# Decoder step on one core: nine pairs of the input projection by seven products instead of eighteen single tiles, with the sums of x formed beside the attention

## The chip, the cores and the metric

The kernel runs on one core of a Trainium2 chip. The metric is the time of one execution on the device in microseconds (us); the median of several runs is given, and one further execution was recorded by the hardware profiler. The engines are named as in the profile: PE (matrix products) with PEld (its weight loads), DVE (vector engine), ACT (scalar engine), POOL (GpSimd) and SP, which here only starts DMA transfers. POOL starts DMA transfers too; such an issue counts as busy time of POOL, one on SP does not count as busy time.

## The reference

One layer of a decoder for 512 prompt tokens and 8 decode tokens (520 in all), width 2048. Everything is float32.

```
def mixer(xn, conv_prev, gla_prev, w_in, conv_w, gate_w2, gate_b, gla_norm_g, w_out, chunk):
    proj = xn @ w_in
    bg, cg, hin, q, k, v, og, glr = jnp.split(proj, [...], axis=-1)
    cu, conv_new = causal_dwconv(cg * hin, conv_prev, conv_w)
    ya = bg * cu
...
    o, s_new = gla_chunked(qh, kh, vh, lf, gla_prev.astype(f32), chunk)
    o = o * lax.rsqrt(var + EPS) * gla_norm_g...
    yb = (o.reshape(...) * jax.nn.silu(og.astype(f32))).astype(xn.dtype)
    out = jnp.concatenate([ya, yb], axis=-1) @ w_out
    return out, conv_new, s_new

def conv_ffn(xn, prev, w_up, conv_w, conv_b, w_down):
    u, v = jnp.split(xn @ w_up, 2, axis=-1)
    cu, new = causal_dwconv(u, prev, conv_w)
    h = jax.nn.silu(cu + conv_b) * v
    return h @ w_down, new
```

`x + mixer(rmsnorm(x))`, then `x + conv_ffn(rmsnorm(x))`, then a last RMSNorm. `bg`, `cg`, `hin` and `og` are 1024 columns of `w_in` each, so eight tiles of 128 columns each.

## The kernel before

**Numbers and tiles.** A float32 product is made of three products of halves: each operand is split into a high part (rounded, written by ACT) and a low part (the rest, written by DVE), and PE adds hi·hi, hi·lo and lo·hi. Activations lie with the width on 128 partitions and the 520 tokens along the row, in two halves of 260 tokens (`HT`).

**Direct groups.** `group()` (L134) makes one tile of 128 output columns from all 16 tiles of the width: 16 tiles × 3 products × 2 token halves = 96 matmuls of 260 columns.

**Seven products.** The output projection ("wo"), the up projection ("up") and the down projection ("down") take a 2 × 2 block (two column tiles or chunks, two halves of the inner width, two token halves) by seven products instead of eight, after Winograd and Strassen. The weights are summed for it on the way (`weights`, `prepare`: three or four DVE additions per group, of which one is in some groups an adding DMA `raw<-raw` that POOL starts), and each of the seven needs its own hi (ACT) and lo (DVE, L1086) of 128 × 1024. The activations are needed in sums too, called forms 1 to 7. One such group is 7 × 24 = 168 matmuls. In "wo" and "down" one operand's forms are written to memory (`g_d`, `f_d`) and loaded back by `load_form` (L612), four loads of 260 KB for each form, into a ring of eight homes (`slots`). In "up" the forms of the normalised x are held in place. The order of the products within a group is `ORDER` = 1, 5, 6, 2, 7, 3, 4.

**Stages.** First x is loaded, transposed and split. Then the attention runs, one head after another; it is cut into steps by generators, and `tick()` runs a step between the projection groups, so that PE alternates between both. Convolution tiles 0 to 3 (three groups each: `cg`, `hin`, `bg`) are made there too. Behind it come convolution tiles 4 to 7 and output gate tiles 0 to 7, twenty direct groups. `mixed_done` takes two finished tiles, forms their sums (`pair_sums`) and stores the forms of the mixer's output to `g_d`: 8 stores of 130 or 260 KB for each pair, all issued on POOL. Then "wo" (two halves of its inner width times four column groups, `(c, g)`), "up" (44 groups), "down", and the last norm.

**What sets the order.** From "wo" on one loop walks over all products i (`order`, j = i % 7 within the group n). It prepares weights two products ahead, finishes the product before (`chunk_finish`, `up_finish`), starts the loads of the next group's weights on SP, and lets generators (`steps`) run their parts at set places. `in_order` keeps POOL's and SP's instructions in program order; every engine works its own queue strictly from the front, so that an instruction that waits holds back all that stand behind it.

**Places that matter here.** `load_residual(g)` (L1225) loads the residual x into the four accumulators `acc[g, q]` of column group g of "wo" with four POOL loads of 260 KB; it is called for g = 0 ahead of the loop, and for the others at j = 4 of the group before. `chunk_finish` adds products onto them on DVE (L1277). The forms of "wo" for c = 0 are loaded between the output gate tiles (14 POOL loads after each of two of them), the first of c = 1 in the first group of "wo", the rest in its fourth group. In "down" `add_residual` (L1230) adds the residual into `acc` by four adding POOL DMAs; it runs at j = 5 of the four groups of c = 1, the last of them at (1, 3), where also the forms of the next c are loaded. With 14 form loads of "down" on POOL and 14 on SP the last "up" group prepares the next stage.

Of the kernel before, what the change touches and what calls it, by code (L numbers as in the profile page):

```python
# [37 lines left out]
def trunk_kernel(  # L38
# [99 lines left out]
    soon, queue = deque(), deque()  # L138
# [26 lines left out]
    def group(w, c0, acts):  # L165
        ps = new_mm()
        ws = [piece(w, k0, 8, c0, P) for k0 in (0, 8)]
        for k0 in range(0, KD, 4):
            span(ps, ws[k0 // 8], acts, k0, k0 // 8 * 8, 4, KD)
            tick()  # L170
        return ps
# [37 lines left out]
    t_d = dp.tile([3, 4, 2, P, T], F32, name="t_d")  # L209
    v_d = dp.tile([NH, NS, DV], F32, name="v_d")  # L210
# [420 lines left out]

    def pair_sums(he, h):
# [9 lines left out]
    with ExitStack() as mix:  # L642
        slots[:4] = [yt1] * 4
        even = {}

        def mixed(k):
# [3 lines left out]
            if k < KD // 2:  # L650
                even[k] = yt1.tile([P, T], F32, tag="yl3", name="ye")
# [31 lines left out]
        with ExitStack() as gl:  # L683
            gp = gl.enter_context(tc.tile_pool(name="gla", bufs=1))
# [254 lines left out]
            for h in range(NH):  # L939
                ps = group(w_in, 3584 + h * P, xa) if h else first[0]  # L940
# [22 lines left out]
            assert not queue, len(queue)  # L963

        yctx = ctx.enter_context(ExitStack())
        slots[4:14] = [yctx.enter_context(tc.tile_pool(name="yt2", bufs=1, side="right"))] * 10
        wxr = yctx.enter_context(tc.tile_pool(name="raw2", bufs=4, side="right"))
        for j in range(4, 8):
            conv_tile(j)

        for j in range(8):
# [7 lines left out]
            if 2 <= j < 6:  # L979
                for x in range(2 * j - 4, min(2 * j - 2, 7)):  # L980
                    load_form("wo", 0, x)

    bctx.close()

# [3 lines left out]
    wx = ctx.enter_context(ExitStack())  # L988
    wxp = wx.enter_context(tc.tile_pool(name="sums", bufs=2))
    slots[14:] = [yctx.enter_context(tc.tile_pool(name="yt3", bufs=1, side="right"))] * 2  # L990
# [10 lines left out]
    def first_tile(kind, g, m):  # L1001

        return 2 * g + 8 * m if kind == "wo" else 4 * g + 2 * m

# [5 lines left out]

    def source(kind, at):
        if kind == "up":
            return lambda m, k: up_source(*at, m, k)
# [37 lines left out]
    groups = [("wo", (c, g)) for c in range(2) for g in range(NG)]  # L1051
# [3 lines left out]
    NW = 7 * 2 * NG  # L1055
# [3 lines left out]
    def begin(n):  # L1059
        kind, at = groups[n]  # L1060

        state[kind, at] = weights(source(kind, at), kind == "up" or at[0] > 0)
# [29 lines left out]
    xq = {}  # L1092
# [26 lines left out]
    def up_finish(i):  # L1119
# [22 lines left out]
        elif r == 3:  # L1142
            add(z2, bk["f"], st["c"])
            if t >= 2:
                nc.vector.tensor_tensor(z2, z2, R[:, HT:], op=ALU.mult)

# [61 lines left out]

    def acc_tag(n):
        return f"x{'hl'[n % 2]}{8 + n // 2}"  # L1210

    def rows_of(d, kind, g, q):

        m, b = first_tile(kind, g, q // 2), q % 2
        return d[m : m + 2, :, b * HT : (b + 1) * HT].rearrange("m p c -> p m c")
# [82 lines left out]
    ssq = [cp.tile([P, T], F32, tag="glr", name="ssq"), R]  # L1298

    def form(f, g):  # L1300

        if f == 1:
            x = pair_tiles(bigA, f"b{g}")
        elif f in (2, 3):
            x = [
                bigA.tile([P, T], F32R, tag=acc_tag(4 * g + q), name="b2")
                for q in ((0, 3) if f == 2 else (1, 2))
            ]
        else:
            k = {5: 0, 4: 4, 6: 8, 7: 12}[f] + g  # L1310
            x = [slots[k].tile([P, T], F32R, tag=f"y{s}{k}", name=f"y{s}{k}") for s in "hl"]
        for j, q in enumerate(zip(*(halves(y) for y in x))):
            xq[f, 2 * g + j] = q
        return x
# [100 lines left out]
    in_order = InOrder(nc.gpsimd.engine, nc.sync.engine)  # L1415
    begin(0)
    load_rest(0)
    load_residual(0)
    prepare(0)
    prepare(1)  # L1420
    steps, seeded = [], {}
    for i, (kind, at, r) in enumerate(order):
# [6 lines left out]
        if i:  # L1429
            (up_finish if order[i - 1][0] == "up" else chunk_finish)(i - 1)  # L1430
# [201 lines left out]
```

## Time and profile before

| | us |
|---|---|
| median of 3 runs (2237.19 to 2238.16) | 2237.39 |
| the profiled execution, its own time | 2237.94 |
| its span (first to last instruction) | 2236.2 |
| PE busy / DVE / ACT / POOL | 2189.3 / 1634.4 / 1049.2 / 459.6 |
| start until the attention | 0 to 70 |
| attention with conv tiles 0 to 3 | 70 to 442 |
| conv tiles 4 to 7, output gate 0 to 7 | 442 to 684.6 |
| "wo" | 685.4 to 856.5 |
| "up" | 856.5 to 1755.6 |
| "down" | 1755.6 to 2166 |
| last part | 2166 to 2236 |

The page has its times in microseconds of the span. In a row of the timeline stand the start, the length of the run of instructions, the engine, the line, the operation, the names (out<-in) and their number; in brackets behind it how long the engine stood idle just before, and what ended that. In a table of windows stand the busy time of each engine in a stretch, with the number of instructions, then the clock that PE was granted (1 is full), the share of the DMA engines' time, and the bytes moved. A group of instructions has its count, its busy time, the mean of one in ns, and the idle time before them.

### The profile page before, as it was taken

To read this page: it belongs to the slowest core of one execution; us is meant where nothing else is said; L and a number is where in the kernel's file an instruction comes from. 1 tells how busy PE (TensorE), PEld (TensorE's weight loads), DVE (VectorE), ACT (ScalarE), POOL (GpSimd) and SP (SyncE) were. 2 spreads that over 40 slices of the span, in tenths; PEclk is the share of its full clock that TensorE was granted. 3 is DMA by queue.
4 is the path that set the end of the run, shared out by engine and by line. 5 is a ranking of instruction groups with operands and counts; after the bars stand their busy time and mean duration, and the time that the engine had idled before them with its cause. 6 is when DMAs were issued, how large, how long until landed. Compare 5 with 4: busy or idle time off the path is not lost.

```text
span 2236.2 us, 43928 instructions
## 1 busy us (share of the span) xinstructions
PE 2189.3 (98%) x17963; PEld 2165.8 (97%) x17963; DVE 1634.4 (73%) x2183; ACT 1049.2 (47%) x1504; POOL 459.6 (21%) x629
## 2 busy tenths in 40 slices
PE   8999999999999998999999999999999999999997
PEld 7998999999999997999999999999999999999997
DVE  5355364544457896888989898898888777777776
ACT  5334334322233485555555555555555554344445
POOL 3023142241333311211312122122121303100100
PEclk9999999999999998999999999999999999999999
DMA  8243353375588699566767667667676869976944
GB/s 248 83 132 98 112 151 107 107 195 129 156 263 253 214 258 288 153 175 165 189 172 183 182 163 195 174 175 185 166 187 194 287 189 224 290 216 179 285 118 152
DMA packets 461239, 413.33 MB, mean 185 GB/s; under 512 B 21177, under 2 KB 417365, under 8 KB 460893
## 3 DMA queue, kind: packets, MB, share of 16 engines
q1 hardware_dynamic: 418353, 285.89, 44.6%
q0 software_dynamic: 41360, 122.40, 21.6%
q8 instruction: 141, 2.31, 0.4%
q10 hardware_dynamic: 1324, 2.23, 0.3%
q14 instruction: 61, 0.50, 0.1%
HBM read 294.13 MB, written 79.25 MB: 167 GB/s over the span
## 4 chain that ended last, share of the span: by engine, by line
PE 84%; DMA 2%; DVE 2%; issue 1%; ACT 1%; SPq 0%; ACTq 0%; DVEq 0%
PE mm L1107 28%; PE mm L134 20%; PE ms L1107 11%; PE x L1259 8%; PE y L1259 8%; PE e L1259 3%; PE f L1259 3%; DMA raw<-in_w_down_dram 1%; PE ms L830 1%; DVE lo L1086 0%; DMA t_d<-t 0%; DVE s L1032 0%; DMA x_d<-acc 0%; PE ms L1533 0%; DMA raw<-in_w_out_dram 0%
## 5 line engine op out<-in xcount | busy, mean ns | idle before, releaser
L1082 ACT ACTIVATE hi<-raw 128x1024 fp32r<-128x1024 f32 x288 | 304.4, 1057 | 215.8 <-issue 71.9
L1107 PE MATMUL mm<-yl,hi 128*128 128x260 f32 x1408 | 398.9, 283 | 3.8 <-DVE yl L118 2.4
L1107 PE MATMUL mm<-yh,hi 128*128 128x260 f32 x1408 | 399.0, 283 | 1.4 <-DMA yh<-t_d 1.4
L1107 PE MATMUL mm<-yh,lo 128*128 128x260 f32 x1408 | 398.0, 283 | 0.0
L1086 DVE TENSOR_TENSOR lo<-raw,hi 128x1024 fp32r<-128x1024 f32 x288 | 351.9, 1222 | 45.9 <-ACT hi L1082 45.6
L1086 DVE TENSOR_TENSOR lo<-s,hi 128x1024 fp32r<-128x1024 f32 x216 | 265.5, 1229 | 116.9 <-ACT hi L1082 111.6
L1082 ACT ACTIVATE hi<-s 128x1024 fp32r<-128x1024 f32 x216 | 228.4, 1057 | 199.5 <-DVE s L1032 74.8
L1107 PEld LDWEIGHTS mm<-yl,hi 128*128 128x128 f32 x1408 | 266.2, 189 | 4.8 <-DVE yl L118 2.7
L1107 PEld LDWEIGHTS mm<-yh,hi 128*128 128x128 f32 x1408 | 265.4, 189 | 1.8 <-DMA yh<-t_d 1.8
L1107 PEld LDWEIGHTS mm<-yh,lo 128*128 128x128 f32 x1408 | 266.4, 189 | 0.0
L1107 PE MATMUL ms<-b,hi 128*128 128x260 f32 x1408 | 258.3, 284 | 0.0
L106 DVE TENSOR_TENSOR lo<-raw,hi 128x1024 fp32r<-128x1024 f32 x112 | 144.6, 1291 | 140.7 <-ACT hi L105 133.6
L105 ACT ACTIVATE hi<-raw 128x1024 fp32r<-128x1024 f32 x112 | 118.1, 1055 | 264.5 <-PE mm L134 220.6
L1107 PEld LDWEIGHTS ms<-b,hi 128*128 128x128 f32 x1408 | 219.0, 190 | 0.0
L1259 PE MATMUL y<-form,hi 128*128 128x260 f32 x1120 | 206.8, 285 | 3.1 <-DVE acc L1277 3.1
L1259 PE MATMUL x<-form,hi 128*128 128x260 f32 x1120 | 205.6, 284 | 3.4 <-DVE acc L1277 2.2
L1107 PE MATMUL ms<-b,lo 128*128 128x260 f32 x704 | 199.6, 284 | 0.0
L1036 POOL DMA_DIRECT2D raw<-raw x64 | 57.2, 894 | 651.0 <-DVE s L1032 481.6
L1032 DVE TENSOR_TENSOR s<-s,raw 128x1024 f32<-128x1024 f32 x144 | 176.0, 1222 | 2.5
L1259 PEld LDWEIGHTS y<-form,hi 128*128 128x128 f32 x1120 | 174.3, 190 | 3.6 <-ACT hi L1082 3.1
L1259 PEld LDWEIGHTS x<-form,hi 128*128 128x128 f32 x1120 | 173.0, 189 | 4.2 <-issue 1.9
L134 PE MATMUL mm<-xh,hi 128*128 128x260 f32 x768 | 160.7, 291 | 3.8 <-ACT xh L120 3.8
(328 smaller groups left out, 5570.5 us busy)
## 6 DMA issues: line engine op xcount, KB each, us to landing
raw<-in_w_up_dram SPq DMA_DIRECT2D x176, 512.0 KB
raw<-in_w_down_dram SPq DMA_DIRECT2D x96, 512.0 KB
raw<-in_w_in_dram SPq DMA_DIRECT2D x92, 512.0 KB
raw<-raw POOLq DMA_DIRECT2D x64, 512.0 KB, 6.2
form<-f_d SPq DMA_DIRECT2D x126, 260.0 KB
f_d<-t POOLq DMA_DIRECT2D x80, 260.0 KB, 5.6
raw<-in_w_out_dram SPq DMA_DIRECT2D x32, 512.0 KB
form<-g_d POOLq DMA_DIRECT2D x56, 260.0 KB, 7.4
```

The costliest lines, as they stand in the source:

```text
L105: nc.scalar.activation(hi, raw, AF.Copy)
L106: nc.vector.tensor_tensor(lo, raw, hi.bitcast(F32), op=ALU.subtract)
L134: nc.tensor.matmul(o, w, xx, start=first and i == 0, stop=last and i == 2)
L830: nc.tensor.matmul(pb[:, c * 64 : (c + 1) * 64], L[:, c, :], rhs[:, c], start=True, stop=True,)
L1032: return lambda: nc.vector.tensor_tensor(out, x, y, op=ALU.add)
L1036: return lambda: nc.gpsimd.dma_start(out, x, accum_op=ALU.add)
L1082: nc.scalar.activation(his[i], src, AF.Copy)
L1086: nc.vector.tensor_tensor(los[i], src, his[i].bitcast(F32), op=ALU.subtract)
L1107: nc.tensor.matmul(st["bank"][b], w[:, k, :], x, start=b not in st["used"] and k == 0 and j == 0, stop=k == 7 and j == 2, skip_group_check ...
L1259: nc.tensor.matmul(ps[:, m, :], w[:, k, m * P : (m + 1) * P], x, start=b not in st["used"] and k == 0 and j == 0, stop=k == 3 and j == 2, ...
```

## The change

Only output gate tiles 0 and 1 stay direct groups behind the attention. The other eighteen tiles (convolution tiles 4 to 7 with three each, gate tiles 2 to 7) become nine pairs of a new kind "mix", which the common loop runs ahead of "wo" with the same `up_product` as "up":

```
+    MIX = (
+        ("ch", 4), ("ch", 5), ("b", 4), ("og", 2), ("ch", 6), ("ch", 7), ("b", 6), ("og", 4),
+        ("og", 6),
+    )
...
-    groups = [("wo", (c, g)) for c in range(2) for g in range(NG)]
+    groups = [("mix", (n,)) for n in range(len(MIX))]
+    groups += [("wo", (c, g)) for c in range(2) for g in range(NG)]
```

For them the forms 4 to 7 of the scaled x are needed. `mixer_sums(g)` makes them for a quarter of the width, in four steps each that run after the groups from head 1 of the attention on. It loads x anew (POOL), scales it (ACT, eight half tiles), forms four sums (DVE) and splits them (ACT, DVE). For g = 0 the results stay on the chip; for g = 1, 2, 3 they go to memory (`mt_d`, 24 POOL stores) and come back through `load_mixer_sums` (24 POOL loads of 260 KB) once the attention's tiles, and for g = 3 the last direct tile's, are free.

```
+    def mixer_sums(g):
+        xg = [tmp()[:, :T] for _ in range(4)]
+        for q, x in enumerate(xg):
+            m = first_tile("mix", g, q // 2)
+            nc.gpsimd.dma_start(two(x), rows_of(xT_d, "mix", g, q))
+            for j, h in enumerate(halves(x)):
+                nc.scalar.activation(h, h, AF.Copy, scale=gmix[:, m + j : m + j + 1])
+        def out(f, t):
+            if g == 0:
+                split(t, *form(f, g))
+            else:
+                stored(t, [mt_d[f - 4, g, x] for x in range(2)], tmp())
+        yield
+        t1, t2 = xg[0], tmp()[:, :T]
+        sub(t1, xg[0], xg[1])
+        minus(t2, t1, xg[3])
+        out(5, t1)
+        yield
...
+    def load_mixer_sums(g):
+        for f in (5, 4, 7, 6):
+            for x, t in enumerate(form(f, g)):
+                nc.gpsimd.dma_start(t.bitcast(F32), mt_d[f - 4, g, x])
...
             for h in range(NH):
+                if h == 1:
+                    extra.extend(mixer_sums(g) for g in range(4))
...
-        for j in range(4, 8):
-            conv_tile(j)
-
-        for j in range(8):
+        for g in (1, 2):
+            load_mixer_sums(g)
+
+        for j in range(2):
...
+    load_mixer_sums(3)
```

`mix_finish` takes the results out of PE's banks (for "b" times the convolution's result, else times R), and `mix_gate` does the rest of a pair in steps during the next group: for "ch" the product of both tiles and the convolution, for "og" the Silu and the product with the attention's output, and for "b" and "og" the sums and stores to `g_d`:

```
+    def mix_gate(n):
+        st = state.pop(("mix", (n,)))
+        u, v = st[2], st[7]
+        what, j = MIX[n]
+        if what == "ch":
...
+        dst, i = g_d[k // 8], k // 2 % 4
+        t21, t34 = pair_sums(u, v)
+        yield 4.5
+        stored(halves(u)[0], [dst[6:7, x, i] for x in range(2)], fh())
+        yield 7
+        stored(v, [dst[4:6, x, i] for x in range(2)], fh())
+        yield 7.5
+        stored(t21, [dst[0:2, x, i] for x in range(2)], fh())
+        yield 10.5
+        stored(t34, [dst[2:4, x, i] for x in range(2)], fh())
```

In the common loop all 28 form loads of "wo", c = 0, move to the last "mix" group, all on POOL; the first residual load comes behind them; one form load of c = 1 moves from the first to the third group of "wo"; and `add_residual` for column group 1 moves from (1, 3) to (2, 2). Four matmuls that only mark banks are added at i = 0.

```
     in_order = InOrder(nc.gpsimd.engine, nc.sync.engine)
+    mult(R2, R, R)
     begin(0)
     load_rest(0)
-    load_residual(0)
...
-        if i == NW:
+        if i in (0, NW):
             x = xq[1, 0][0]
             for ps in [bank() for _ in range(4)]:
                 nc.tensor.matmul(ps[:, :HT], x[:, :P], x, start=True, stop=True)
...
-            if c == 0 and g == 0 and j == 0:
+            if c == 0 and g == 2 and j == 0:
                 load_form("wo", 1, 0)
...
-        if kind == "up" and at[0] == NF - 1:
+        if 7 * n in (NM - 7, NU - 7):
             for x in {1: (0, 1), 2: (2, 3), 4: (4, 5), 6: (6,)}.get(j, ()):
-                load_form("down", 0, x)
+                load_form(groups[n + 1][0], 0, x)
+        if i == NM - 1:
+            load_residual(0)
...
-            if c == 1 and j == 5:
-                add_residual((g + 2) % NG)
+            if j == 5 and (c, g) in ((1, 0), (1, 1), (1, 2), (2, 2)):
+                add_residual({0: 2, 1: 3}.get(g, c - 1))
```

Three places of the instruction order follow. First POOL behind the attention. Before the change the eight stores of the pair of convolution tiles 2 and 3 (`g_d`) are followed by form loads for "wo":

```order
L630 DMA g_d0_119<-t_4935 128x2x260
L612 DMA form_6812<-g_d0_119 128x2x260
L612 DMA form_6816<-g_d0_119 128x2x260
L612 DMA form_6820<-g_d0_119 128x2x260
L612 DMA form_6824<-g_d0_119 128x2x260
L612 DMA form_6972<-g_d0_119 128x2x260
```

With the change the same stores are followed by 24 loads from `mt_d`, eight for each of g = 1, 2, 3; the names yh, yl with a number are the places of the hi and lo parts. The last eight, for g = 3, are:

```order
L697 DMA yh3_5433<-mt_d_122 128x520
L697 DMA yl3_5434<-mt_d_122 128x520
L697 DMA yh7_5437<-mt_d_122 128x520
L697 DMA yl7_5438<-mt_d_122 128x520
L697 DMA yh15_5441<-mt_d_122 128x520
L697 DMA yl15_5442<-mt_d_122 128x520
L697 DMA yh11_5445<-mt_d_122 128x520
L697 DMA yl11_5446<-mt_d_122 128x520
```

The pair `yh3`, `yl3` is form 5 of g = 3: it stands seventeenth and eighteenth among the loads.

Second, POOL ahead of "wo". Before, the four loads of the residual (`acc`) follow the stores of one gate pair, and the 28 form loads stand between the gate tiles, in two runs of 14:

```order
L630 DMA g_d1_120<-t_7122 128x2x260
L1225 DMA acc_7566<-xT_d_116 128x2x260
L1225 DMA acc_7567<-xT_d_116 128x2x260
L1225 DMA acc_7568<-xT_d_116 128x2x260
L1225 DMA acc_7569<-xT_d_116 128x2x260
L612 DMA form_7630<-g_d1_120 128x2x260
L630 DMA g_d1_120<-t_7514 128x260
```

With the change they stand at the end of a run of 28 form loads with four stores among them, of which these are the last:

```order
L615 DMA form_7651<-g_d0_119 128x2x260
L615 DMA form_7715<-g_d0_119 128x2x260
L615 DMA form_7717<-g_d0_119 128x2x260
L615 DMA form_7719<-g_d0_119 128x2x260
L615 DMA form_7721<-g_d0_119 128x2x260
L1395 DMA acc_7723<-xT_d_116 128x2x260
L1395 DMA acc_7724<-xT_d_116 128x2x260
L1395 DMA acc_7725<-xT_d_116 128x2x260
L1395 DMA acc_7726<-xT_d_116 128x2x260
L633 DMA g_d1_120<-fh_7772 128x2x260
```

So `acc` is now the last of 36 issues that all belong to the last "mix" group.

Third, DVE in the first group of "wo". The first two additions onto `acc` (product 5, bank y) stand between the low parts (`lo`) of the weights for the coming products. Before:

```order
L1086 TENSOR_TENSOR lo_7699<-raw_7559,hi_7696 128x1024
L1277 TENSOR_TENSOR acc_7567<-acc_7567,y_7639 128x520
L1277 TENSOR_TENSOR acc_7569<-acc_7569,y_7639 128x520
L1086 TENSOR_TENSOR lo_7730<-s_7557,hi_7728 128x1024
L1277 TENSOR_TENSOR acc_7566<-acc_7566,e_7597 128x520
```

With the change:

```order
L1170 TENSOR_TENSOR lo_7856<-raw_7411,hi_7853 128x1024
L1447 TENSOR_TENSOR acc_7724<-acc_7724,y_7796 128x520
L1447 TENSOR_TENSOR acc_7726<-acc_7726,y_7796 128x520
L1234 TENSOR_TENSOR t_7596<-t_7596,t_7778 128x520
L1234 TENSOR_TENSOR t_7653<-t_7653,t_7779 128x520
L1170 TENSOR_TENSOR lo_7889<-s_7409,hi_7887 128x1024
```

The place is the same, and between the additions and the next `lo` now stand two products of the last gate pair.

More of the change, by code (lines that the diff above doesn't have):

```diff
@@ L170, in group @@
             tick()
+        if extra and next(extra[0], extra) is extra:
+            extra.popleft()
         return ps
@@ L209, in trunk_kernel @@
     t_d = dp.tile([3, 4, 2, P, T], F32, name="t_d")
+    mt_d = dp.tile([4, 4, 2, P, T], F32, name="mt_d")
     v_d = dp.tile([NH, NS, DV], F32, name="v_d")
@@ L650, in mixed @@
             if k < KD // 2:
[L651 removed]
+                even[k] = evp[0].tile([P, T], F32, tag="ye", name="ye")
             else:
@@ L1145, in up_finish, with mult, mix_finish @@
                 nc.vector.tensor_tensor(z2, z2, R[:, HT:], op=ALU.mult)
+    R2 = cp.tile([P, T], F32, tag="glr", name="R2")
+    conv_z = {}
+    def mult(out, x, y):
+        nc.vector.tensor_tensor(out, x, y, op=ALU.mult)
+    def mix_finish(i):
+        kind, (n,), r = order[i]
+        st = state[kind, (n,)]
+        bk = st["bank"]
+        what, j = MIX[n]
+        if r == 1:
+            copied(st, "e")
+        elif r == 6:
+            copied(st, "f")
+        elif r == 5:
+            st["c"] = tmp()[:, :HT]
+            nc.scalar.activation(st["c"], bk["c"], AF.Copy)
+        elif r in (2, 7):
+            st[r] = tmp()[:, :T]
+        if r in (2, 3):
+            u = halves(st[2])
+            f = halves(conv_z[j] if what == "b" else R)
+            if r == 3:
+                add(u[1], bk["f"], st["c"])
+                if what != "ch":
+                    mult(u[1], u[1], f[1])
+            elif what == "ch":
+                nc.scalar.activation(u[0], bk["e"], AF.Copy)
+            else:
+                mult(u[0], bk["e"], f[0])
+        elif r in (7, 4):
+            v = halves(st[7])
+            if r == 7:
+                add(v[1], bk["a"], st["c"])
+            if what == "b":
+                f = halves(conv_z[j + 1])
+                if r == 7:
+                    mult(v[1], v[1], f[1])
+                else:
+                    mult(v[0], bk["a"], f[0])
+            elif r == 4:
+                nc.scalar.activation(v[0], bk["a"], AF.Copy)
@@ L1295, in chunk_finish @@
             onto(2, "a", ALU.subtract)
[L1298 to L1314, printed above, removed]
+    ssq = []
     def projected(g):
```

124 lines of the change are left out of this document (94 added, 30 removed).

## The prediction

> **What bounds the kernel now.** I read the page first, for the engine that is full.
>
> ```profile
> span 2236.2 us, 43928 instructions
> PE 2189.3 (98%) x17963; PEld 2165.8 (97%) x17963; DVE 1634.4 (73%) x2183; ACT 1049.2 (47%) x1504; POOL 459.6 (21%) x629
> PE 84%; DMA 2%; DVE 2%; issue 1%; ACT 1%; SPq 0%; ACTq 0%; DVEq 0%
> ```
>
> PE is busy for 98% of the span and carries 84% of the chain of waits. So time goes down only if PE gets fewer matmuls, and every gain is lost again where PE is made to wait. The second view is therefore the table of windows, by stage.
>
> ```profile
> 441.90:684.60 242.70, 242.70 (x2019) 242.51 (x2017) 114.78 (x174) 66.32 (x82) 70.33 (x95) 1.00 0.68 188
> 685.40:856.50 171.10, 165.31 (x1349) 164.40 (x1349) 154.22 (x176) 101.51 (x145) 47.71 (x64) 0.99 0.85 247
> 856.50:1755.60 899.10, 893.46 (x7407) 891.68 (x7407) 787.43 (x1045) 488.71 (x719) 184.11 (x259) 0.99 0.70 184
> ```
>
> In the stage that is changed (first row) PE never stands still: 242.7 us for the last group of convolution tile 3 and the twenty direct groups, 21 in all, so 11.56 us for one. DVE is busy there for 47%. In "up", which already works by seven products, DVE is busy for 88%, and PE still loses only 5.6 us in 899. The third view is the timeline of PE at one product of two successive "up" groups.
>
> ```profile
> 938.12 0.41 PE L1107 MATMUL ms<-b,hi 128*128 128x260 f32 x2
> 958.24 0.41 PE L1107 MATMUL ms<-b,hi 128*128 128x260 f32 x2
> ```
>
> A group of seven products takes 20.12 us, one product 2.87.
>
> **The matmuls.** Eighteen direct groups go, 18 × 11.56 = 208.1 us; nine pairs come, 9 × 20.12 = 181.1 us. That is **−27.0 us**, all of it on PE and so on the path. Per pair DVE gets seven `lo` and three additions, the same as in "up", and in place of the gate of "up" the work of one or two finished tiles.
>
> ```profile
> L1086 DVE TENSOR_TENSOR lo<-raw,hi 128x1024 fp32r<-128x1024 f32 x176 | 214.9, 1221 | 11.4 <-ACT hi L1082 11.3
> L1032 DVE TENSOR_TENSOR s<-s,raw 128x1024 f32<-128x1024 f32 x88 | 107.6, 1223 | 1.5
> L1155 DVE TENSOR_TENSOR t<-t,R 128x520 f32<-128x520 f32 x41 | 28.5, 694 | 0.0
> ```
>
> Ten of 1.22 us make 12.2; behind them come about 8 us of pieces of 0.69 (whole tiles) and 0.43 (halves) in a gate pair, less in the others: 20.2 against 20.12. In "up" DVE's busy time is 787.4 / 44 = 17.9 us a group, and PE waits for almost none of it. So I cost DVE here at nothing, with 0 to +3 us for the three gate pairs.
>
> **The moved residual.** The largest stall of the last third stands in "down" at (1, 3).
>
> ```profile
> 1942.00 0.39 PE L1259 MATMUL y<-form,lo 128*128 128x260 f32 x1 [3.23 <-DVE lo L1086]
> 1945.70 0.48 PE L1259 MATMUL x<-form,hi 128*128 128x260 f32 x2 [0.80 <-DVE acc L1277]
> 1939.59 1.23 DVE L1032 TENSOR_TENSOR s<-raw 128x1024 f32<-128x1024 f32 x1 [6.12 <-DMA raw<-in_w_down_dram]
> 1915.47 5.21 POOL L1230 DMA_DIRECT2D acc<-x_d  x4
> 1936.00:1942.00 6.00, 2.77 (x24) 2.56 (x23) 2.42 (x3) 2.12 (x2) 0.62 (x1) 1.00 1.08 347
> ```
>
> DVE waits for weights that are late, with the DMA engines full (share 1.08). The four adding DMAs at 1915 fall into the loads of 28 forms. Moved to (2, 2), they meet no such run: **−4.0 us** (3.23 + 0.80). If the forms alone fill the DMA, it is 0.
>
> **The four extra matmuls** at i = 0 cost 4 × 0.12 = +0.5 us.
>
> **From the direct groups to the pairs.** 24 loads stand on POOL where before stood 14. The rows of before, at the same place:
>
> ```profile
> 464.75 2.13 POOL L612 DMA_DIRECT2D form<-g_d  x3
> 470.41 1.49 POOL L612 DMA_DIRECT2D form<-g_d  x2 [3.53 <-DMA g_d<-t]
> 480.00 0.72 POOL L612 DMA_DIRECT2D form<-g_d  x1 [0.64 <-DMA form<-g_d]
> form<-g_d POOLq DMA_DIRECT2D x56, 260.0 KB, 7.4
> ```
>
> The fourteenth load starts at 480.0. The wait of 3.53 is for stores to land: an issue of POOL waits for an older DMA, so that few are in flight. Form 5 of g = 3 is the eighteenth load: 480.0 + 4 × 0.9 = 483.6, and with 0.7 to issue and 7.4 to land it is there at 491.7. PE needs it three quarters through the second product. The first pair starts at 441.9 + 3 × 11.56 = 476.6; with 0.5 + 2.87 + 2.15 that is 482.1. So PE stalls for **+9.5 us**. If issues alone set the pace (0.72 each from 464.75), it is 3; at the slowest pace seen for POOL loads (1.22, next rows), 12. The third and later forms come ahead of their products once this one is there.
>
> **From the pairs to "wo".** Let the last pair start at t0. Its first loads for "wo" wait for product 2 (t0 + 5.75). There follow 36 issues: 28 form loads, 4 stores, 4 residual loads. Two paces are seen:
>
> ```profile
> 748.57 0.72 POOL L612 DMA_DIRECT2D form<-g_d  x1 [35.32 <-PE y L1259]
> 772.92 0.72 POOL L612 DMA_DIRECT2D form<-g_d  x1 [2.55 <-DMA form<-g_d]
> 698.63 0.72 POOL L1225 DMA_DIRECT2D acc<-xT_d  x1
> 711.80 1.45 POOL L1225 DMA_DIRECT2D acc<-xT_d  x2 [0.50 <-DMA acc<-xT_d]
> ```
>
> 28 form loads from 748.57 to 772.92, 0.87 each, beside weights at the same rate as here; and twelve residual loads from 698.63 to 713.25, 1.22 each. By the first the residual's last load is issued at t0 + 5.75 + 36 × 0.87 = 37.1 and lands some 7.2 later, at t0 + 44.3. Who waits? Before, the residual was loaded early and its first use came 10.3 us after the start of "wo" (685.4):
>
> ```profile
> 679.90 2.83 POOL L1225 DMA_DIRECT2D acc<-xT_d  x4 [9.27 <-PE mm L134]
> 695.73 1.30 DVE L1277 TENSOR_TENSOR acc<-acc,y 128x520 f32<-128x520 f32 x2
> ```
>
> Now that use would be at t0 + 20.1 + 10.3 = 30.4, and DVE stands 14 us at it. Behind it in DVE's queue stand two products of the gate pair and the `lo` of the sixth product of "wo", so PE runs on until t0 + 20.1 + 5 × 2.89 = 34.6 and stops. DVE then needs 1.3 + 1.4 + 1.2 = 3.9 us after 44.3, so PE goes on at 48.2: **+13.5 us**. With issues alone (0.72 each) it is 8; at 1.22 each 26.
>
> **In the attention.** Per quarter DVE gets eight operations of 0.65 us, ACT twelve, POOL ten issues of 0.7 us. The stage's row leaves room:
>
> ```profile
> 70.00:442.00 372.00, 367.33 (x2969) 354.86 (x2969) 182.35 (x302) 142.13 (x216) 93.51 (x108) 1.00 0.41 115
> 201.84 1.11 PE L830 MATMUL ms<-L 128*128 128x64 f32 x8 [2.32 <-DVE L L773]
> 196.39 1.37 DVE L743 TENSOR_TENSOR_SCAN bc<-ones,t 128x128 f32<-128x128 f32 x4
> 197.84 2.76 POOL L224 TENSOR_TENSOR e<-bc 128x256 f32<-128x256 f32 x3 [6.31 <-DVE bc L743]
> ```
>
> But at the start of head 1 PE already waits along DVE scan, POOL `e`, DVE `L`. In the order of the changed kernel DVE's operation ahead of the scan waits for a store of the sums to land, whose buffer it takes over, and POOL has three store issues (2.1 us) ahead of `e`. The wait for landing I put at 2 to 3 us. That is **+4 us**, between 0 (landed in time) and 12 (all three heads).
>
> **The clock.** After stalls the profile shows a lower granted clock, but not after each:
>
> ```profile
> 850.00:856.00 6.00, 4.63 (x24) 4.46 (x24) 5.97 (x7) 4.61 (x10) 2.11 (x3) 0.72 1.07 362
> 868.00:874.00 6.00, 3.30 (x14) 2.93 (x14) 4.74 (x6) 3.83 (x7) 0.85 (x1) 0.54 1.09 352
> 874.00:880.00 6.00, 6.00 (x34) 6.00 (x34) 3.68 (x6) 3.43 (x7) 0.85 (x1) 0.61 1.14 270
> ```
>
> Around 851 the loss is 6 × 0.28 = 1.7 us; from 868 to 880 it is 5.1 us; after the 4.0 us at 1942 the row above has 1.00, none. For the two new long stalls I take 1.7 each, **+3.4 us**, between 0 and 10. The Trainium skill ("TensorE: Matmul & The Clock Gate", section "Part 1: The HAM clock gate") halves the clock after an idle window of about 3.4 us and restores it after as long a busy one, which for two stalls gives an estimate of 3.4 us too; by it the 2.9 us at 850 would be free and the 4.0 us at 1942 not, and both rows are the other way.
>
> **Sum.** −27.0 − 4.0 + 0.5 + 9.5 + 13.5 + 4.0 + 3.4 = −0.1 us. Against the profiled execution (2237.94, span 2236.2 and 1.7 around it) that is 2237.8; the median of before lies 0.55 lower, so I forecast **2237 us: no change**. Of 27 us saved on PE, two queues on POOL give back 23.
>
> **Rivals.**
> *Faster: the transitions are nearly hidden.* If POOL's loads go at their issue time, the stalls are 3 and 8, and if the attention keeps its slack and the clock its speed, the sum is −27 − 4 + 0.5 + 3 + 8 = −19.5: 2218; with half of that effect 2227. For it: 0.72 us is what an issue takes in every row. Against: in both runs of loads the pace was 0.87 or more, because older DMAs have to land first. The Trainium skill ("DMA: Bandwidth & Descriptors", section "Anatomy of one DMA — SWDGE (gpsimd) path") has a fixed 2.0 us and the bytes at 436 GB/s, an estimate of 2.6 us for such a load against 7.4 measured here; by it the last landing would come 4.8 us earlier in both places, the sum would be −9.7 and the time 2228, and it counts as a part of this rival. Chance 0.33.
> *Slower: one queue, residual last.* If the 36 issues go at 1.22 us, as the twelve residual loads did with the DMA engines full (share over 1.0 at 850 and 1936), PE stalls 26 in place of 13.5: +12.4, 2250. It decides for slower from a pace of about 1.0 us: 36 × (1.0 − 0.87) = 4.7. For it: in these 45 us weights, forms, stores and sums all move at once. Against: the run at 748 moved weights and 28 forms at 0.87, with a share of 0.93:
>
> ```profile
> 748.00:773.00 25.00, 25.00 (x210) 25.00 (x209) 19.64 (x21) 10.83 (x13) 17.38 (x25) 1.00 0.93 288
> ```
>
> Chance 0.24.
> *Slower: DVE or the attention.* Three gate pairs at +1, the heads at +12 instead of +4: +11, 2248. Chance 0.06.
> *It doesn't do what it says.* The order of the changed kernel shows nine groups of 168 matmuls in place of eighteen of 96, so this has no chance to speak of.
>
> **How the numbers follow.** Forecast 0.37, within 2232 to 2243; faster 0.33, 2218 to 2232; slower 0.30 in all, 2242 to 2256. A measurement of this kernel can tell about 0.2% from no change, 4.5 us. The range leaves out a tenth at either end: 2221 to 2253. Faster by over 0.2% 0.35, within 0.33, slower 0.32: the edges of the forecast's own range go to both sides.
>
> **What would show it.** Right: PE at 20.1 us for each pair; one stall of some 10 us on a DMA of `mt_d` in the second product of the first pair; one of some 13 us in the first group of "wo", where DVE waits for a DMA of `acc`; no stall at (1, 3) of "down". Wrong: no wait of DVE for `acc` (then the faster rival), POOL's spacing at over 1.0 us (the slower), waits for `lo` within the pairs, or stalls in heads 2 and 3.

## The result, and the profile after

The changed kernel takes 2254.54 us (median of 4 runs, 2252.56 to 2255.3), the kernel before beside it 2237.29 (2236.44 to 2238.16): a ratio of 1.0076, 95% interval 1.0058 to 1.0093. It is **slower by 17 us**, where no change was forecast; the time lies 1.5 us above the range's upper end. The profiled execution took 2252.56 us, its span 2250.8, so 14.6 us more than the span of before.

The page of the changed kernel, its first lines and the chain by engine:

```profile
span 2250.8 us, 43866 instructions
PE 2171.4 (96%) x17751; PEld 2143.3 (95%) x17751; DVE 1739.4 (77%) x2290; ACT 1112.7 (49%) x1625; POOL 490.7 (22%) x687
PE 83%; DMA 6%; DVE 5%; ACT 2%; issue 2%; POOL 1%; SPq 1%; ACTq 0%; DVEq 0%; POOLq 0%
```

PE has 212 recorded matmuls fewer (216 fewer in the pairs, four more that mark banks) and is busy 17.9 us less, and yet the span is longer: PE's idle time rose from 46.9 to 79.4 us, and the chain now has 6% of DMA and 5% of DVE in place of 2% each. Where that time lies is read from the stages. The boundaries in the table are starts of PE's first matmul of a stage; "attention" ends with the start of the last group of convolution tile 3 (441.2 before, 457.3 after).

| stage | before | after | difference | as forecast |
|---|---|---|---|---|
| start and attention | 441.2 | 457.3 | +16.1 | +4.0 |
| from there to "wo" | 244.3 | 232.2 | −12.1 | −27.0 + 0.5 + 9.5 + 1.7 = −15.3 |
| "wo" | 171.0 | 188.3 | +17.3 | +13.5 + 1.7 = +15.2 |
| "up" | 899.2 | 898.3 | −0.8 | 0 |
| "down" | 410.7 | 405.4 | −5.2 | −4.0 |
| last part | 69.9 | 69.2 | −0.7 | 0 |
| sum | | | +14.6 | −0.1 |

Windows of the changed kernel: attention, the rest of the direct groups, pairs, "wo".

```profile
70.00:457.90 387.90, 371.90 (x2967) 357.26 (x2968) 206.85 (x334) 163.86 (x264) 122.45 (x148) 0.99 0.48 138
457.90:501.00 43.10, 35.00 (x290) 34.76 (x289) 16.86 (x27) 12.45 (x16) 23.59 (x37) 0.94 0.72 225
501.00:689.40 188.40, 184.88 (x1517) 183.97 (x1517) 158.85 (x202) 92.81 (x134) 43.94 (x65) 0.99 0.74 199
689.40:877.80 188.40, 167.70 (x1348) 165.96 (x1349) 156.75 (x182) 104.50 (x150) 67.22 (x92) 0.96 0.91 273
```

PE's matmuls in the attention are as many as before (2967, before 2969), in a stretch 15.9 us longer. "wo" too has the same work in 188.4 us, with the DMA engines busy for 0.91 of the time (before 0.85). The stalls themselves, in PE's timeline:

```profile
136.99 1.41 PE L883 MATMUL ms<-s,qm 128*32 128x256 f32 x4 [2.05 <-DVE s L870]
209.97 1.97 PE L897 MATMUL ms<-L 128*128 128x64 f32 x8 [6.03 <-DVE L L840]
279.08 0.77 PE L774 MATMUL ms<-idn,v 128*128 128x128 f32 x4 [2.47 <-DVE v L492]
309.13 1.10 PE L897 MATMUL ms<-L 128*128 128x64 f32 x8 [2.06 <-DVE L L840]
326.67 1.02 PE L883 MATMUL ms<-s,qm 128*32 128x256 f32 x4 [1.83 <-DVE s L870]
501.01 0.56 PE L1190 MATMUL mm<-bh,hi 128*128 128x260 f32 x1 [8.12 <-DVE t L492]
702.63 0.80 PE L1429 MATMUL x<-form,hi 128*128 128x260 f32 x2 [6.91 <-ACT e L1453]
721.38 0.58 PE L1429 MATMUL f<-form,lo 128*128 128x260 f32 x1 [7.19 <-DVE lo L1170]
```

Five stalls in the attention, where before there were 2.32 us at 201.84 and 1.8 in two others; one ahead of the first pair; two at the start of "wo". No stall of 3 us is left in "down". In the attention (70 to 442 before, 70 to 457.9 now) PE's waits grow from 5.3 to 16.7 us in all. The other 4.6 us are busy time of the same matmuls: behind two of the five stalls the granted clock is low, at 1.00 behind the other three.

```profile
136.00:142.00 6.00, 5.01 (x25) 3.95 (x26) 5.55 (x9) 1.25 (x2) 3.12 (x2) 0.72 0.44 133
210.00:216.00 6.00, 6.00 (x28) 6.00 (x29) 5.85 (x10) 2.71 (x4) 5.37 (x7) 0.50 0.22 75
```

What DVE does while PE stands still is seen ahead of the stall at 279:

```profile
275.20 1.15 ACT L117 ACTIVATE t<-t 128x520 fp32r<-128x520 f32 x2
275.86 2.83 DVE L118 TENSOR_TENSOR t<-t 128x520 fp32r<-128x520 f32 x2 [6.62 <-ACT t L117]
278.61 0.75 DVE L492 TENSOR_TENSOR v<-mm,R 128x260 f32<-128x260 f32 x2
```

DVE stands idle for 6.6 us with the low part of a sum at the front of its queue. That piece waits for its high part, which ACT writes only at 275.20, behind work for the norm of a head (L532 to L535, 270.48 to 275.3). The copy `v` that PE waits for stands behind it. The idle time of DVE ahead of the lines that make sums and low parts of activations (L586, L592 and L118) is 35.1 us in the attention, and 0.0 before; of the 35.1 some 2.5 belong to the pair of convolution tiles.

At the start of "wo" the waits behind these two are seen on ACT, DVE and POOL:

```profile
698.93 0.64 ACT L117 ACTIVATE fh<-t 128x520 fp32r<-128x520 f32 x1 [9.52 <-DMA g_d<-fh]
715.53 0.69 DVE L1447 TENSOR_TENSOR acc<-acc,y 128x520 f32<-128x520 f32 x1 [8.34 <-DMA acc<-xT_d]
718.27 0.70 DVE L1447 TENSOR_TENSOR acc<-acc,y 128x520 f32<-128x520 f32 x1 [2.05 <-DMA acc<-xT_d]
699.38 7.83 POOL L615 DMA_DIRECT2D form<-g_d  x11 [4.04 <-DMA g_d<-fh]
674.00:689.00 15.00, 14.98 (x126) 14.77 (x124) 14.36 (x21) 6.69 (x9) 10.49 (x15) 1.00 1.04 319
```

ACT waits 9.5 us until a store of `fh` has landed and its tile is free, and holds back the copy `e` that PE needs; DVE then waits 10.4 us for `acc`. The window ahead of them has the DMA engines full (share 1.04, 319 GB/s). Behind the stalls at 501 and 703 the granted clock is low:

```profile
499.00:505.00 6.00, 3.38 (x14) 3.11 (x15) 5.66 (x7) 1.58 (x2) 1.79 (x4) 0.50 1.06 379
703.00:716.00 13.00, 11.19 (x76) 10.98 (x75) 4.66 (x5) 3.17 (x4) 9.90 (x14) 0.83 1.01 336
```

### The profile page after: what moved, and what is told of

Read it like the earlier page. It is cut to its first block, busy times and chain, and to the rows that moved or that the text cites. A ratio compares the mean times of both kernels' runs of the same rounds, so it can differ in the third digit from the quotient of the medians.

```text
span 2250.8 us, 43866 instructions
## 1 busy us (share of the span) xinstructions
PE 2171.4 (96%) x17751; PEld 2143.3 (95%) x17751; DVE 1739.4 (77%) x2290; ACT 1112.7 (49%) x1625; POOL 490.7 (22%) x687
## 4 chain that ended last, share of the span: by engine, by line
PE 83%; DMA 6%; DVE 5%; ACT 2%; issue 2%; POOL 1%; SPq 1%; ACTq 0%; DVEq 0%; POOLq 0%
PE mm L1190 33%; PE ms L1190 13%; PE mm L134 11%; PE y L1429 8%; PE x L1429 8%; PE f L1429 3%; PE e L1429 3%; DMA t<-o_d 1%; DMA yl<-t_d 1%; DVE lo L106 1%; PE ms L897 1%; DVE lo L1170 1%; DMA vb<-v_d 1%; DMA form<-g_d 1%; DMA s<-in_state_gla_dram 1%
## 5 line engine op out<-in xcount | busy, mean ns | idle before, releaser
L1190 PE MATMUL mm<-yl,hi 128*128 128x260 f32 x1696 | 478.5, 282 | 3.5 <-DVE yl L118 2.8
L1190 PE MATMUL mm<-yh,lo 128*128 128x260 f32 x1696 | 480.1, 283 | 1.0 <-DVE lo L1170 1.0
L1190 PE MATMUL mm<-yh,hi 128*128 128x260 f32 x1696 | 479.9, 283 | 0.7 <-DMA yh<-t_d 0.5
L1170 DVE TENSOR_TENSOR lo<-s,hi 128x1024 fp32r<-128x1024 f32 x243 | 298.3, 1228 | 126.6 <-ACT hi L1166 121.1
L1166 ACT ACTIVATE hi<-s 128x1024 fp32r<-128x1024 f32 x243 | 257.2, 1059 | 221.3 <-DVE s L1112 85.2
L1190 PEld LDWEIGHTS mm<-yl,hi 128*128 128x128 f32 x1696 | 319.5, 188 | 4.4 <-DVE yl L118 3.0
L1190 PEld LDWEIGHTS mm<-yh,lo 128*128 128x128 f32 x1696 | 319.5, 188 | 1.2 <-DVE lo L1170 1.2
L1190 PEld LDWEIGHTS mm<-yh,hi 128*128 128x128 f32 x1696 | 319.4, 188 | 1.3 <-DMA yh<-t_d 0.7
L1429 PE MATMUL x<-form,lo 128*128 128x260 f32 x560 | 159.2, 284 | 0.0
L1429 PE MATMUL y<-form,lo 128*128 128x260 f32 x560 | 158.3, 283 | 0.0
```

What stands on the lines that cost most here:

```text
L1166: nc.scalar.activation(his[i], src, AF.Copy)
L1170: nc.vector.tensor_tensor(los[i], src, his[i].bitcast(F32), op=ALU.subtract)
L1190: nc.tensor.matmul(st["bank"][b], w[:, k, :], x, start=b not in st["used"] and k == 0 and j == 0, stop=k == 7 and j == 2, skip_group_check ...
L1429: nc.tensor.matmul(ps[:, m, :], w[:, k, m * P : (m + 1) * P], x, start=b not in st["used"] and k == 0 and j == 0, stop=k == 3 and j == 2, ...
```

## The experiments

Each run had the kernel before beside it on the same chip; its median was between 2234.1 and 2235.0 us there, so times are read as ratios or from the stages (the ratio of the changed kernel, 1.0076, would be some 2251.5 us there). The attention is given from PE's first group of it to the last group of tile 3: 370.8 us before, 386.9 changed. How far a stage varies by itself is seen where a run leaves it untouched: attention of the changed kernel 385.3 to 388.4 (five profiles), from there to "wo" 231.8 to 233.0 (six), "wo" 188.1 to 190.3 (nine). Less than that isn't read as an effect.

**The sums taken out of the attention.** First, is it the sums at all that lengthen it?

```
             for h in range(NH):
                 if h == 1:
-                    extra.extend(mixer_sums(g) for g in range(4))
+                    load_mixer_sums(0)
...
-                nc.gpsimd.dma_start(t.bitcast(F32), mt_d[f - 4, g, x])
+                nc.gpsimd.dma_start(t.bitcast(F32), xT_d[4 * (f - 4) + g])
```

> The sums of x are not formed during the attention; all four quarters of the forms 4 to 7 are filled with unscaled x instead (8 more POOL loads at head 1), so the outputs are not the reference's. If the sums are what makes the attention 16.1 us longer (70 to 457.9 in place of 70 to 441.9), its end comes back to 442 to 444 and the time falls from 2254.5 to about 2239. If the cause lies elsewhere (the even tile's new place, other tile places), the end stays beyond 450 and the time above 2247.

Measured: 2236.77 us, ratio 1.0009 (0.9999 to 1.0019); the attention takes 370.3 us, the other stages stay as in the changed kernel (232.4 from there to "wo", "wo" 188.3). So the sums cost 16.6 us, and with them at nothing the change would just come out even: what pairs save and "down" gains goes to the stalls around the pairs.

**A ring of their own.** The temporary tiles come from a ring of eight that the attention uses too. In the changed kernel DVE stood still for 8.7 us at 183 with a sum at the front of its queue, until POOL was done with a temporary tile:

```profile
191.59 0.70 DVE L586 SCALAR_TENSOR_TENSOR t<-t 128x520 f32<-128x520 f32 x1 [8.71 <-POOL t L231]
```

```
+        def own():
+            if g == 0:
+                return tmp()[:, :T]
+            k, s = ring[ringn[0] % 8]
+            ringn[0] += 1
+            return yt1.tile([P, T], F32R, tag=f"y{s}{k}", name=f"y{s}{k}").bitcast(F32)
-        xg = [tmp()[:, :T] for _ in range(4)]
+        xg = [own() for _ in range(4)]
...
-                    extra.extend(mixer_sums(g) for g in range(4))
+                    extra.extend(mixer_sums(g) for g in (1, 2, 3, 0))
```

> The sums for g = 1, 2, 3 take their tiles from the eight homes that wait for the forms of g = 0, not from the ring of eight temporary tiles that the attention uses too; g = 0 is formed last. Work and transfers are the same. Theory of the ring (an instruction of the one waits until the other has given a tile back): the attention ends at 442 to 448, time 2239 to 2246. Theory of the work (the issues on POOL and the pieces on ACT and DVE stand in the chain themselves): the end stays at 453 to 460, time 2250 to 2256.

Measured: 2264.05 us, ratio 1.0132 (1.0110 to 1.0153), the attention takes 399.3, 12 us longer still. What the theory of the ring forecast did not come. The run changes more than the ring, though: with free tiles the sums are issued earlier, g = 0 is formed last, and the stalls move with them. PE's timeline of this run has two at head 0 that were not there.

```profile
104.91 1.12 PE L783 MATMUL ms<-idn,v 128*128 128x128 f32 x4 [7.58 <-DVE v L492]
132.86 1.94 PE L906 MATMUL ms<-L 128*128 128x64 f32 x8 [5.83 <-DVE L L849]
220.85 1.37 PE L906 MATMUL ms<-L 128*128 128x64 f32 x8 [2.32 <-DVE L L849]
```

At the start of head 1 (last row) only the 2.32 us of before are left, since few sums remain there. The shared ring had held the sums back; what it costs by itself isn't shown.

**Which part of the sums.** Two runs divide them: transfers alone, and everything but the stores.

```
# transfers only
+        for n, (f, q) in enumerate(((5, 0), (4, 3), (7, 2), (6, 1))):
+            for x in range(2):
+                nc.gpsimd.dma_start(mt_d[f - 4, g, x], xg[q])
# no stores
-                stored(t, [mt_d[f - 4, g, x] for x in range(2)], tmp())
+                split(t, tmp()[:, :T].bitcast(F32R), t.bitcast(F32R))
```

> Only the transfers of the sums stay in the attention (12 loads of x, 24 stores to mt_d, all issued on POOL, and 8 loads straight into the forms of g = 0); the 32 scalings and 24 other pieces on ACT and the 32 on DVE are left out, so the forms hold unscaled x and the outputs are not the reference's. If POOL's issues ahead of the attention's own POOL work are the cause, the attention (70 to the last group of tile 3) stays 10 or more us over the 370 us of before, time 2248 or more. If DVE's and ACT's pieces are, it comes to 370 to 374, time 2237 to 2241.

> The sums are loaded, scaled, summed and split as in the change, but the 24 stores to mt_d are left out, and the later loads take unscaled x, so the outputs are not the reference's. If ACT and DVE are the cause, the attention stays 12 to 17 us over before (382 to 387), time about 2251 to 2255. If the stores on POOL are, it falls to 370 to 376, time 2238 to 2243. Both together would show as a share in each run.

Measured: transfers alone 2243.93 us (ratio 1.0043), the attention 375.0, so 4.2 longer than before; without the stores 2251.59 us (1.0080), 384.8, so 14.0 longer. The second run still has the twelve loads of x. (ACT has 48 pieces in all, 32 scalings and 16 splits; the expectation counts eight too many.) The waits of PE in the attention, first of the one, then of the other:

```profile
PE ms L887 <- DVE L L830: 5.8, 1, 5.8
```

```profile
PE ms L883 <- DVE s L870: 5.0, 4, 2.1
PE mm L134 <- DVE lo L106: 4.8, 2, 4.7
PE ms L774 <- DVE v L492: 2.5, 1, 2.5
PE ms L897 <- DVE L L840: 2.3, 1, 2.3
```

The transfers alone make one long stall, at the start of head 1. The pieces on ACT and DVE make five of 1.8 us or more, spread over the heads, and one of them stands at the same place: the 4.7 us for `lo`, which DVE writes behind two sums' low parts and the scan.

```profile
204.44 0.59 PE L134 MATMUL mm<-bh,lo 128*128 128x260 f32 x1 [4.66 <-DVE lo L106]
```

The 2.3 us for `L` in this run are not at the start of head 1 but at head 2 (306.9). So either half of the sums delays head 1, and the two don't add up there; their sum, 18.2, is a little over the 16.1 of the whole. DVE's idle time ahead of the lines L586, L592 and L118 is 34.3 us without the stores, and 2.6 with transfers alone, which are those of the convolution tiles.

**Later, and less of it.** Two runs move or lighten the same sums, a third does both.

```
# late
-                if h == 1:
+                if h == 3:
-        if extra and next(extra[0], extra) is extra:
-            extra.popleft()
+        for _ in range(2):
+            if extra and next(extra[0], extra) is extra:
+                extra.popleft()
# unsplit
-                stored(t, [mt_d[f - 4, g, x] for x in range(2)], tmp())
+                nc.gpsimd.dma_start(mt_d[f - 4, g, 0], t)
...
+    def split_mixer_sums(f):
+        for g in (1, 2, 3):
+            hi, lo = unsplit[f, g]
+            split(lo.bitcast(F32), hi, lo)
```

> The same sums, with two steps after each group from head 3 on in place of one from head 1 on, so that the starts of heads 1 and 2 are free of them. Theory: the sums cost only where they stand ahead of a head's start, where PE waits for the chain DVE scan, POOL e, DVE L; the attention falls to 372 to 380, time 2240 to 2248. Rival: they cost the same wherever they stand (own amount of work), attention 384 to 390, time 2252 to 2256.

> Same result as the change, another way: the sums for g = 1, 2, 3 go to memory unsplit (12 stores and 12 loads in place of 24 and 24) and are split into hi and lo after they come back, in the first pair. That takes 12 pieces each from ACT and DVE and 12 issues from POOL out of the attention, and half the bytes from its end. Theory (each piece ahead of a head's chain costs, and bytes cost behind the attention): attention 386.9 to 376 to 380, from its end to wo 232.2 to 226 to 229, time 2238 to 2244. Rival: the splits make DVE late in the first pair, and what the attention gains is lost there, time 2250 or more.

> The same with the sums formed from head 3 on. Placing them late gained 3.4 us in the attention with split sums; if the two gains add up, attention 372 to 376 and time 2234 to 2240; if both act on the same pieces, no better than the unsplit run.

Measured: late 2251.5 us (1.0077, 1.0064 to 1.0091), the attention 386.0, so 0.9 less (the 3.4 of the last expectation count in that the stage began 2.5 us earlier); unsplit 2249.49 (1.0062, 1.0045 to 1.0078), 383.9; both 2253.62 (1.0081, 1.0066 to 1.0096), 386.4. Late keeps the start of head 1 as it was, but then PE waits at other places, ahead of the last head above all (the 2.3 us for `L` are the wait of before):

```profile
PE ms L971 <- DVE S L984: 5.4, 1, 5.4
PE ms L898 <- DVE L L841: 3.9, 3, 2.3
PE ms L775 <- DVE v L493: 3.6, 1, 3.6
```

The 5.4 us for `S` are of the same kind as the stall at 279. DVE stands with a sum at its front that waits for ACT's scaling, and `S` stands a few pieces behind:

```profile
328.73 0.70 DVE L593 TENSOR_TENSOR t<-t 128x520 f32<-128x520 f32 x1 [8.80 <-ACT t L674]
```

So the later place is no cheaper, and my theory that only the heads' starts are dear falls; the earlier place, in the run with a ring of its own, was dearer. Nor do DVE's waits give the price by their sum: the late run has 11.4 us of them in place of 35.1 and costs about as much. It matters what PE needs of the pieces that stand behind. A third of the pieces on ACT and DVE less (24 of 80) together with twelve stores less saves 3.0 us at most, about the stage's own spread; both together save nothing that can be told. From the attention's end to "wo" the unsplit run needs 232.2 us like the change: half the loads there gain nothing.

**The start of "wo": queue or bytes?** The prediction took POOL's queue for the cause, with `acc` at its end. Three runs test that: `acc` first, half of the form loads on SP, and half the bytes.

```
# residual first
+        if i == NM - 7:
+            load_residual(0)
...
-        if i == NM - 1:
-            load_residual(0)
# split
-                first = kind == "wo" or c == 0 and x == 1
+                first = kind == "wo" and c or c == 0 and x == 1
# half the bytes (the same in load_mixer_sums)
+        once = kind == "wo" and c == 0
-        for x in range(2):
+        for x in range(1 if once else 2):
...
-            parts_.append(tiles)
+            parts_ += [tiles] * (2 if once else 1)
```

> The four residual loads of group 0 are issued ahead of the 28 form loads, at the start of the last pair. Theory of the prediction (residual last in the queue): DVE's wait for acc (8.3 and 2.1 us) goes and with it the stall of 7.2 us at 721; wo shrinks from 188.3 to about 180, time about 2246. Rival (the whole queue is late, and the stores of the last pair stand behind the forms): ACT's waits for a store of fh stay or grow, wo stays at 185 or more, time 2251 to 2255.

> Half of the 28 form loads for wo (the hi parts) are issued on SP, half on POOL, as it is done for down. If POOL's queue sets both stalls at the start of wo, both go: wo 188.3 to 172 to 175, time 2239 to 2242. Rival (the DMA engines are full, share over 1.0, whoever issues): one of the stalls stays, or the weights on SP come late behind the forms; wo stays above 182, time above 2248.

> Of the sums (mt_d) and of the first 7 forms of wo only the hi parts are loaded, and stand in for the lo parts too, so the outputs are not the reference's: 12 loads in place of 24 ahead of the pairs, 14 in place of 28 ahead of wo, all on POOL. Theory of the bytes (the DMA engines are full: about 17 MB fall due in 34 us, and 340 GB/s move): the stalls of 6.9 and 7.2 us at the start of wo go, wo 188.3 to 172 to 175, and the one of 8.1 us ahead of the pairs shrinks below 3; time about 2232 to 2237. The run with split queues left POOL half the issues and all the bytes and gained 2 us in wo; if here too the stalls stay, it is neither.

Measured: residual first 2262.55 us (ratio 1.0125), "wo" 191.8 and the stretch ahead of it 237.4, together 429.2 in place of 420.5. DVE's wait for `acc` and the stall at 721 are gone, as the theory has it, but PE now waits for the forms, and longer for the copy `e` behind ACT:

```profile
PE x L1429 <- ACT e L1453: 8.3, 1, 8.3
PE x L1429 <- issue: 5.7, 1, 5.7
PE x L1429 <- DMA form<-g_d: 5.2, 2, 4.3
```

Split queues 2252.13 us (1.0078), "wo" 186.1, 2.2 us better, with 233.6 ahead of it, so nothing in sum. `acc` and the store come earlier, but one stall of 13.3 us takes the place of the two: DVE waits for a gate load (`o_d`) on SP, which now stands behind 14 form loads there, while the DMA engines are as full as before.

```profile
718.46 0.70 DVE L1234 TENSOR_TENSOR t<-t 128x520 f32<-128x520 f32 x1 [7.13 <-DMA t<-o_d]
703.00:710.00 7.00, 5.61 (x47) 5.40 (x46) 1.49 (x2) 1.21 (x2) 2.96 (x5) 1.00 1.04 359
710.00:722.00 12.00, 0.14 (x1) 0.14 (x1) 3.42 (x5) 2.95 (x4) 0.71 (x1) 0.60 1.03 330
```

Half the bytes: 2234.94 us (1.0004, 0.9994 to 1.0014), "wo" 177.3, 11.0 us better but short of the forecast 172 to 175, with stalls of 1.1 and 4.3 us left; the stretch ahead of it is 4.4 us shorter too. (The stages are those of the profiled execution, which at 2241.4 was the longest of ten.) With half the issues taken off POOL (split) "wo" gained 2.2, with half the bytes and the same 14 issues left on POOL 11.0: the stalls go with what is moved, in a stretch where the DMA engines have nothing left, and not with POOL's queue. Half the bytes are half the DMAs here too; no run separates these two. What can't be moved in time comes late, whichever stands last.

In the same run the stall ahead of the first pair was 5.9 us in place of 8.1, with 12 loads in place of 24. But it was 6.0 in the run without the sums, which has all 24, so that isn't shown to be an effect of the loads.

**More time ahead of the pairs.**

```
-        for j in range(2):
+        for j in range(4):
             og, e, on = tmp(), mixed(8 + j), tmp()
...
-        ("ch", 4), ("ch", 5), ("b", 4), ("og", 2), ("ch", 6), ("ch", 7), ("b", 6), ("og", 4),
-        ("og", 6),
+        ("ch", 4), ("ch", 5), ("b", 4), ("ch", 6), ("ch", 7), ("b", 6), ("og", 4), ("og", 6),
```

> Gate tiles 2 and 3 stay direct groups too, so four direct groups and eight pairs follow the attention; two more direct groups of 11.56 us and one pair of 20.12 us fewer cost 3.0 us of PE. The 24 loads of sums and the first pair's weights get 23 us more. Theory (the transfers at the end of the attention lack time): the stall of 8.1 us ahead of the first pair and the half clock behind it go, about 11 us, so from the attention's end to wo 232.2 becomes 223 to 226 and the time about 2246. Rival (the first pair's weights are late for a wait that moves with it): 232 to 236, time 2253 to 2258.

Measured: 2255.4 us (ratio 1.0099), 233.6 from the attention's end to "wo"; so of the 3.0 us that it costs on PE some 1.6 came back, hardly more than the stage's own spread, and nothing beyond. PE's waits in that stretch:

```profile
PE mm L134 <- ACT hi L105: 4.0, 1, 4.0
PE ms L1189 <- DVE lo L1169: 3.8, 1, 3.8
```

The stall ahead of the first pair is gone, but two others stand in its place: weights of a direct group and of the first pair. In the changed kernel too the wait at 501 is one for weights: the addition that stands ahead in DVE's queue needs the tile `s` and two weight tiles, which lie where the attention's tiles were. SP could issue these loads only at 479.9, when a store out of that space had landed, and they arrived at 499:

```profile
479.87 1.39 SPq L1109 DMA_DIRECT2D raw<-in_w_in_dram  x2
499.30 1.23 DVE L1112 TENSOR_TENSOR s<-raw 128x1024 f32<-128x1024 f32 x1 [19.25 <-issue]
```

How much of these 19 us is the loads of `mt_d` beside them, and how much the late start, isn't settled: halving the loads shows no clear gain, more time moved the stall. No run changed the place of the tiles.

**The moved residual alone.**

```
-            if c == 1 and j == 5:
-                add_residual((g + 2) % NG)
+            if j == 5 and (c, g) in ((1, 0), (1, 1), (1, 2), (2, 2)):
+                add_residual({0: 2, 1: 3}.get(g, c - 1))
```

> The kernel before with only the last adding residual load moved from (1, 3) to (2, 2) of down. The stage table of the changed kernel has down at 405.4 in place of 410.7; if that is the move alone, this kernel is 4 to 5.3 us faster than before (about 0.2%) and the stall of 3.2 us at 1942 is gone. Rival: the gain in down comes from other tile places, then 0.

Measured: 2229.26 us (11 runs) against 2234.73, ratio 0.9977 (0.9968 to 0.9986); "down" takes 406.1 us. The two longest waits of PE from 1750 to 2160 in this run:

```profile
PE mm L134 <- issue: 0.8, 1, 0.8
PE x L1259 <- ACT t L1136: 0.5, 1, 0.5
```

This kernel, the one before with one call moved, is faster than both.

## Why the prediction was wrong

Two terms failed. The pieces of the sums on ACT and DVE were put at nothing in the attention, which makes most of the error; and the pace of the loads ahead of "wo" was read too fast from a row. Two sums came out near what was measured by luck.

- **The matmuls** (−27.0): right. The nine pairs take 188.4 us from 501.0 to 689.4, 7.3 more than 9 × 20.12, most of them half clock and three short waits in the first pair; PE had 216 matmuls fewer in them. DVE is no bound within the pairs: PE waits there for 3.1 us in all, at the start.
- **In the attention** ("+4 us, between 0 and 12"): this is the step that failed, and it makes 12.1 of the 14.7 us of error. It measured +16.1, four times as much and outside its bounds. The prediction counted the pieces on ACT and DVE as free, because the stage's row left room (DVE busy 182 of 372 us). The runs show them to be the larger part: 14.0 us without any store, 4.2 with transfers alone, 0 with neither. At two stalls (279, and 332 of the late run) the rows show how: DVE stands idle with a sum at the front of its queue, and what PE needs waits behind. That the other stalls come about in the same way isn't shown one by one. No term stood here for the half clock behind the stalls: (1 − clock) over the two windows shown above is an estimate of 4.7 us, against 1.7 before (0.72 from 202 to 208), so 3.0 of the 4.6 us of longer busy time.
- **The one place that it priced**, the start of head 1, was priced by two waits that did not come, a store's landing and three store issues. The stall there is 3.7 us longer than before (6.03 in place of 2.32), near the +4, and that is luck: DVE has no wait for a landing ahead of the scan, and POOL's three issues are over before `bc` is there. POOL's `e` starts 1.4 us after the scan, as before (196.39 and 197.84); the scan itself is 7.6 us later.

```profile
204.01 1.36 DVE L810 TENSOR_TENSOR_SCAN bc<-ones,t 128x128 f32<-128x128 f32 x4
203.11 1.81 POOL L633 DMA_DIRECT2D mt_d<-t  x3 [4.75 <-ACT t L117]
205.45 3.85 POOL L227 TENSOR_TENSOR e<-bc 128x256 f32<-128x256 f32 x4 [0.53 <-DVE bc L810]
```

- **From the direct groups to the pairs** (+9.5 and 1.7 for the clock, in sum with the rest −15.3): measured −12.1, so 14.4 us lost against 11.2. That the size is near is luck: PE stops ahead of the first product, not in the second, and for weights, not for form 5. Form 5 of g = 3 landed at 502.4, so it would have been late too, by an estimate of 4 us (the first pair would have started at 492.9 without the stall, and needs it 5.5 us later), but the weights were later.
- **From the pairs to "wo"** (+13.5 and 1.7): measured +17.3. DVE did wait for `acc`, at the place that was named, for 10.4 us in place of 14; PE's stall behind it was 7.2 us in place of 13.5. The wait of ACT for `fh`, which makes the first stall of 6.9, was not seen at all, and only the two together, 14.1 us, come near the 13.5. That `acc` stands last does set this one wait, but not the loss: with `acc` first the two stages are 8.7 us longer, with the issues divided nothing is gained in sum, with half the bytes "wo" is 11.0 us shorter. The count that fits is one of what is moved: 7.5 MB of forms and 1.1 of the residual beside weights and stores, at some 320 to 360 GB/s.
- **The pace** of 0.87 us was misread. Between 748.57 and 772.92 stand 24 form loads, not 28 (the window's 25 instructions of POOL are these and one adding DMA; the other four stand at the start of "wo"), so the row gives 1.06 from start to start. With 1.06 the same sum comes to +20.4 in place of +13.5, and the forecast to 2244. In the changed kernel the 36 issues took from 673.89 to 710.93, 1.03 each.
- **The moved residual** (−4.0): right, −5.2 in the changed kernel; by itself the one call gives −5.5.
- **The clock** (+3.4) was taken too low. The granted clock is 0.57 from 501 to 507, 0.55 from 703 to 708 and 0.56 from 721 to 725; (1 − clock) over these stretches is an estimate of 2.6 and 4.0 us for the two places, against 1.7 each. The 4.0 us at 1942 that the prediction takes for one stall are two, of 3.23 and 0.80 us with some 3 us of matmuls between, so that row doesn't tell what follows a stall of 4 us.
- **The rivals.** The time lies with "slower", to which 0.32 was given. Both mechanisms named there came about in part: the attention beyond its +12 (0.06), and a pace over 1.0 us, from which the rival of one queue (0.24) was to decide for slower, though not its 1.22 and not its stall of 26 us.

## What to carry to other kernels

An engine that is half idle over a stage isn't free there: work put ahead of a latency chain in a queue that is worked from the front can delay the chain each time, and should be priced by how long it will wait at the front of that queue and what stands behind it, not by the stage's mean load. To place it later did not help here. Where a burst of loads makes others late, count the bytes that fall due against what the DMA engines moved in the fullest windows, before reordering the queue; when they are full, order and issuing engine only chose who waits here. When a pace is read from a row, count the instructions in it. And measure the small edits of a large change alone: here the one call that was moved along the way is the only change measured that made the kernel before faster.

## What the runs showed of the hardware

With the DMA engines full (share 0.97 from 479.9 to 485, 1.05 to 1.07 from there to 504), an issue on SP that takes 0.37 us elsewhere took 3 to 11 us, with no wait on a semaphore counted in it:

```profile
481.31 3.35 SPq L1149 DMA_DIRECT2D raw<-in_w_in_dram  x1
493.19 11.14 SPq L1044 DMA_DIRECT2D t<-o_d  x1
```

Loads behind on SP are held up by that as well, which the split run paid for. An issue on POOL of 260 KB costs by its shape: 0.54 us for a plain 128 × 520 (`mt_d`), 0.71 for two blocks of 260 (`g_d`), though both move the same bytes; a store of 130 KB in one block takes 0.55. And a low clock did not follow each stall in the attention: it was 0.50 for the 6 us behind a stall of 6.03 us and 0.72 behind one of 2.05, but 1.00 behind stalls of 2.47 and 2.06.
